# A two-layer hybrid backbone on one core: attention's float32 products issued in two groups of key blocks, a seventh place for a block, and another price of array changes in the kernel's clock model

## The chip, the core and the metric

The kernel runs on one core of a Trainium2 chip. The core has TensorE (PE, matrix products, into PSUM), VectorE (DVE), ScalarE (ACT), GpSimd (POOL) and SyncE (SP, which issues the DMAs). Each engine works through its own list of instructions in order and waits on semaphores for the others. The metric is the device time in microseconds of one execution.

## What is computed

Two layers on 1024 latent and 256 context tokens of width 1024, all in float32. In each layer one input projection feeds three groups of heads, whose outputs are gated, joined and projected out. The group that the change touches is windowed attention with 8 query heads of width 64 in two key-value groups, blocks of 128 tokens:

```python
def one_block(args):
    qn, kn, vn, mn = args
    s_loc = jnp.einsum('bqhgd,bkhd->bhgqk', qn, kn).astype(F32)
    s_loc = jnp.where(mn, s_loc, NEG_INF)
    s_ctx = jnp.einsum('bqhgd,bchd->bhgqc', qn, kc).astype(F32)
    s_sink = jnp.broadcast_to(sink_l[None, :, :, None, None], s_ctx.shape[:-1] + (1,))
    p = jax.nn.softmax(jnp.concatenate([s_sink, s_ctx, s_loc], axis=-1), axis=-1)
    p_ctx = p[..., 1:1 + nc].astype(vn.dtype)
    p_loc = p[..., 1 + nc:].astype(vn.dtype)
    return (jnp.einsum('bhgqc,bchd->bqhgd', p_ctx, vc)
            + jnp.einsum('bhgqk,bkhd->bqhgd', p_loc, vn))
...
y_l = jnp.concatenate([a_l, b_l, c_l], axis=-1) @ w_out
xl = xl + gate[:, None] * y_l
```

A latent block attends to the two context blocks and to itself and its neighbours, so to four or five key blocks; in layer 0 the two context blocks attend to the two context blocks alone. The other groups are a convolution module (31 taps, on DVE) and a gated linear attention in two directions (GLA).

## The kernel before

The program is written by a planner that runs when the kernel is built. Each piece of work is a generator, a "lane". It yields what it needs next: a flag, a free buffer, a free PSUM bank, or a time on the planner's clocks. `loop` takes the ready lane of the best priority and lets it issue; if none is ready, the planner's clock moves on. The clocks are kept by `Model`: `issue` adds the cost of each instruction to its engine's clock and notes when its result may be read. So the costs of the model decide the order of all engines, and the order stays as planned when the chip takes other times. `pick` also chooses by these clocks which engine does a copy or a subtraction. All instructions pass through one helper, so that the profile gives line 43 for all of them; they are told apart by the names of tiles.

A matmul that names a `tile_position` uses a part of the array's 128 columns. Three kinds do: PV of attention (64 columns), the GLA's states (32) and outputs and masks (64), and the modulation vectors (32). All other matmuls and the transposes use 128. In the model a matmul with `tile_position` costs its share of the columns and 29 ns.

Attention runs in units of one query block and one key-value group: 20 in layer 0, 16 in layer 1. `u_run` takes four probability buffers P of 644 columns, issues the scores of four heads (`u_score`), and each head's mask, maximum and exponential run in `u_head`. Then the rows are scaled, and for each key block four transposes (one a head) bring the probabilities into a PSUM bank. `u_ev` copies the bank into a place "PT" of 512 columns, on ACT or DVE. There are six such places, all in tile H1_0, made by `h1_keep`, which also holds the values `vst`. `u_pv` multiplies the transposed probabilities with the values, one key block after the other, into one bank O, two matmuls a block (output partitions 0 to 63 and 64 to 127), and frees the place after each block. A float32 matmul shows as two in the profile, so one block as four.

The SM buffers (14, and one more that holds the rotary table for a while) are divided during attention (`rsv`): nine wide ones of 644 columns for P and the mask, and the narrow ones SM9 to SM14 of 512 columns for the preparation of queries and keys, the gates and the output.

`out_tiles` is the output projection, in two lanes (`par` 0 and 1) that take every second block. Each splits the mixed activations of its block in a leading part `hi` and a correction `lo` (float32 as two parts). Lane 0 keeps half of `lo` in `ml`, a part of tile H1_1, for all blocks but the last four, and needs one SM buffer then; lane 1 needs two. Towards the end of layer 0 the tokens are normalised for layer 1 (`x_next`, `part_h`), which then starts with the first projection groups.

Of the kernel before, what the change touches and what calls it, by code (L numbers as in the profile page):

```python
# [30 lines left out]
def is_ap(x):  # L31
    return hasattr(x, "tensor") and hasattr(x, "ap")


class Engine:


    def __init__(self, model, name, e):
        self._m, self._n, self._e = model, name, e
# [9 lines left out]
class Model:  # L49
# [3 lines left out]
    def __init__(self, nc):  # L53
        self.nc = nc
        self.clock = dict(pe=0.0, act=0.0, dve=0.0, pool=0.0, sp=0.0, ring=0.0, dma=0.0)
        self.mem, self.memo = {}, {}
        self.end = self.cold = 0.0
        for n, a in (("pe", "tensor"), ("act", "scalar"), ("dve", "vector"), ("pool", "gpsimd"), ("sp", "sync")):
            setattr(self, a, Engine(self, n, getattr(nc, a)))

# [56 lines left out]
    def issue(self, e, op, a, k):  # L117
        out = a[0]
        outs = [x for x in (out, k.get("accum_out")) if is_ap(x)]
        ins = [x for x in list(a[1:]) + [v for n, v in k.items() if n != "accum_out"] if is_ap(x)]  # L120
        c = self.clock
        t = c[e]
        w = 2 if e == "pe" else 0
        rp, wp = [self.part(x) for x in ins], [self.part(x) for x in outs]
        for m, b in rp:
            t = max(t, m[w, b].max())
        for m, b in wp:
            t = max(t, m[1, b].max())
            if e != "pe":
                t = max(t, m[0, b].max())  # L130
        if e == "sp":
            c["sp"] = t + 50
            c["ring"] = max(c["ring"], t) + 475
            c["dma"] = max(c["dma"], c["ring"] + 625) + out.free_size() * 4 * out.partition_size() / 360.0
            t = c["dma"]
            near, far = 908, 1100
        else:
            x = self.cost(e, op, out, ins, len(outs) - 1)
            if e == "pe":
                if "tile_position" in k:  # L140
                    x = x * out.partition_size() / 128.0 + 29
                if t - c[e] > 3000 or t < 3000:
                    self.cold = t + 3800
                if t < self.cold:
                    x *= 2
            t += x
            c[e] = t
            near, far = (200, 200) if e == "pe" else (150, 370)
        for m, b in rp:
            m[1, b] = np.maximum(m[1, b], t + near)  # L150
        for m, b in wp:
            m[0, b] = np.maximum(m[0, b], t + near)
            m[2, b] = np.maximum(m[2, b], t + far)
        self.end = max(self.end, t + far)
# [10 lines left out]
class Hybrid:  # L165
# [71 lines left out]
    def memory(self):  # L237
# [10 lines left out]
        self.rt = self.tile(f"SM{NSM}", 512, F32)  # L248
        self.slots["PT"], self.slots["SF"] = [], []
        self.rsv, self.kept = False, None  # L250
# [30 lines left out]
    def get(self, cls, dt=F32, wide=False):  # L281
        x = min(self.choice(cls, wide), key=lambda y: (y[1] not in self.narrow and y[0] > 0, y[0]))
        self.slots[cls].remove(x)
        t = x[1] if cls in ("PT", "SF") else self.tile(x[1], 512 if x[1] in self.narrow else self.size[cls], dt)
        self.where[self.key(t)] = (cls, x[1], t)
# [258 lines left out]
    def h1_keep(self):  # L544
# [4 lines left out]
        for k in range(6):  # L549
            p = x[:, 768 + 512 * k:1280 + 512 * k]  # L550
            self.slots["PT"].append((self.nc.touched(p), p))

# [654 lines left out]
    def attn_start(self, l):  # L1207

        nc = self.nc
        self.kst = self.HC[:, 0:3072].rearrange("p (v s t) -> p v s t", v=2, s=2)  # L1210
        self.Q = [x.rearrange("p (h t) -> p h t", h=8) for x in (self.HC[:, 3072:4096], self.H1[1][:, 0:1024])]
        self.ml = self.H1[1][:, 3072:3584].rearrange("p (a b t) -> p a b t", a=2, b=2)
        yield self.need("SM", 1, 0, True), tuple(f"{x}{l}.{i}" for x in ("kv", "q0", "q1") for i in range(2, NT))
        self.rope_free()
        self.amask = self.sm(640)
        self.rsv = True
        nc.sync.dma_start(self.amask, self.I["amask"])
        self.go(self.gate_rows(l), 3)
        ctx = [0, 1] if l == 0 else []
        blocks = list(range(2, NT)) + ctx if CTXL else ctx + list(range(2, NT))  # L1220
        prev = None
        for n, i in enumerate(blocks):
            for kv in range(2):
                u = self.unit(l, n, i, kv, prev)
                self.units.append(u)
                u.lane = self.go(self.u_run(u), 2 + 0.01 * len(self.units))
                prev = u
        self.outs = self.go(self.out_proj(l, blocks), 8)
        done = set()
        for n, i in enumerate(blocks):  # L1230
            for t in self.keys(i):
                if t not in done:
                    done.add(t)
                    yield f"kv{l}.{t}", lambda: 0.0 if self.pre < 4 else None
                    self.pre += 1
                    self.go(self.kv_prep(l, t, blocks.index(t - 3) if t >= 6 else None), 1)
            yield f"q0{l}.{i}", f"q1{l}.{i}", lambda: 0.0 if self.pre < 4 else None
            self.pre += 1
            self.go(self.q_prep(l, n, i), 1)
# [69 lines left out]
    def unit(self, l, n, i, kv, prev):  # L1309
# [3 lines left out]
        u.keys = self.keys(i)  # L1313
        u.P, u.PT = {}, {}
        return u

    def u_run(self, u):
# [28 lines left out]
        for q in range(len(u.keys)):  # L1346
            yield self.bank_need("tr"), self.need("PT")
            tp = self.bank_get("tr")
            PT = self.get("PT")
            for h in range(4):  # L1350
# [49 lines left out]
    def u_pv(self, u):  # L1400

        nc = self.nc
        nk = len(u.keys)
        bank = None
        for q in range(nk):
            yield lambda: u.PT[q][1] if q in u.PT else None, (0.0 if q else self.bank_need("ac"))
            if q == 0:
                bank = self.bank_get("ac")
                O = bank[:, 0:256].rearrange("p (a t) -> p a t", a=2)
            PT = u.PT[q][0]  # L1410
            p4 = PT.rearrange("p (a b t) -> p a b t", a=2, b=2)
            for b in range(2):
                nc.tensor.matmul(O[64 * b:64 * b + 64], self.vst[:, self.kslot(u.keys[q]), u.kv], p4[:, :, b], start=(q == 0),
                                 stop=(q == nk - 1), tile_position=(0, 64 * b))
            self.free(PT)
        yield None, tuple(f"bg{u.l}.{2 + 2 * u.kv}.{j}.{self.hslot(u.i)[0]}" for j in (0, 1))
        c = col(u.i * 128)
        g = self.mix(slice(2 + 2 * u.kv, 4 + 2 * u.kv), slice(c, c + 128))
        nc.vector.tensor_tensor(g, O, g, op=ALU.mult)
        self.free(bank)  # L1420
        self.flag(f"u{u.key}")
# [52 lines left out]
    def out_tiles(self, l, blocks, par, lanes):  # L1474
        yield
        for n, i in list(enumerate(blocks))[par::2]:
            early = par == 0 and n < len(blocks) - 4
            lanes[par].prio = 8 + 0.01 * n
            if l == 0 and n >= len(blocks) - 2:
                a = 256 + 256 * par  # L1480
                hi = self.HC[:, 0:3072].rearrange("p (a c) -> p a c", a=4)[:, :, a:a + 256].rearrange("p a (b t) -> p a b t", b=2)
                free = f"sc{l}.{len(blocks) - 3}"
            else:
                a = 1024 + 1024 * par
                hi = self.H1[1][:, a:a + 1024].rearrange("p (a b t) -> p a b t", a=4, b=2)
                free = f"h1out{l}"
            yield (self.need("SM", 2 - early, 1), f"u{l}.{n}.0", f"u{l}.{n}.1", free, f"gb{l}",
                   f"ln{l}{self.hslot(i)[0]}", self.rest(hi), (self.rest(self.ml) if early else 0.0))
            m = [self.sm(512, F32R) for _ in range(2 - early)]
            lo = ([self.ml] if early else []) + [x.rearrange("p (a b t) -> p a b t", a=2, b=2) for x in m]  # L1490
            o = col(i * 128)
            for h in range(2):
                yield
# [144 lines left out]
    def phase_bc(self, l):  # L1638
        nc = self.nc
        yield self.attn  # L1640
        yield f"sc{l}.{NT - 1 if l == 0 else NT - 3}"
        self.rsv = False
        self.cap = dict(mm=0, tr=CAPC[0], ac=CAPC[1], md=MDC if l == 0 else 0)
        if l == 0:
            self.go(self.rope_load(), 3)
            for i in list(range(2, NT)) + [0, 1]:
                self.go(self.x_next(i), 1 + 0.01 * ((i - 2) % NT))
        yield tuple(u.lane for u in self.units), f"ml{l}.0", f"ml{l}.1"
        self.slots["SF"] = []
        if l == 0:  # L1650
            self.slots["PT"] = []
            self.h1_new(0, F32R)
        self.flag(f"hfree{l + 1}1")
        self.free(self.amask)
        yield self.outs
        self.flag(f"hfree{l + 1}0")
        self.flag(f"hfree{l + 1}2")
# [189 lines left out]
```

## Time and profile before

| | us |
|---|---|
| median of 3 runs (1331.18 to 1339.85) | 1332.32 |
| the profiled execution | 1333.02 |
| its span, first to last instruction | 1331.2 |
| TensorE busy | 1256.9 |
| DVE, ACT, POOL busy | 831.9, 563.6, 463.7 |
| PV, all 640 matmuls | 86.7 |

The profiled execution is one run with the hardware profiler on. A busy engine is one with an instruction in it; matmuls overlap each other, so that the time from one start to the next is shorter than the duration shown. In the order of time, neighbouring equal instructions are merged into one row with their count: start, us from the first start to the last end, engine, line, operation, output and inputs by tile names, shapes, count, and in brackets idle time ahead with its releaser. "128\*64" are rows and columns of the array in use. A wait is put down to the semaphore that came last.

### The profile page before, as it was taken

What the parts mean: (1) busy time and instruction counts of PE and PEld (TensorE: products, weight loads), DVE (VectorE), ACT (ScalarE), POOL (GpSimd) and SP (SyncE); (2) the same over time, 40 slices, a digit from 0 to 9 for tenths busy, and PEclk for the clock granted to TensorE, in tenths of its full rate; (3) what the DMA queues carried; (4) which work ended last, traced back from release to release, by engine and by line L of the source; (5) the groups of instructions that cost most, each with busy time, mean ns of one, the idle gap of its engine ahead of it and who ended that gap; (6) DMA issues with size and microseconds to landing.
All of it is one profiled execution on the core that took longest, in us unless ns stands there. A gap on an engine that the chain in (4) does not pass through costs nothing. (4 is left out here: it accounts for less than half of the span.)

```text
span 1331.2 us, 24579 instructions
## 1 busy us (share of the span) xinstructions
PE 1256.9 (94%) x9518; PEld 1064.3 (80%) x9518; DVE 831.9 (62%) x1566; ACT 563.6 (42%) x1279; POOL 463.7 (35%) x615
## 2 busy tenths in 40 slices
PE   5999988999999999999999799979999999999997
PEld 3678877888897777776899789878888777888877
DVE  5846896886364355466545578897854646675463
ACT  3721441254324465566513441521443346646541
POOL 1410054744132333534300231074751334445320
PEclk9999998999999999999999899999999999999999
DMA  9443114223014333323232521124231121231012
GB/s 330 147 153 104 48 41 105 60 68 96 25 32 143 101 98 95 97 76 104 82 118 88 198 74 61 41 58 110 80 83 32 50 85 45 66 117 53 1 64 72
DMA packets 113237, 116.49 MB, mean 88 GB/s; under 512 B 38464, under 2 KB 81760, under 8 KB 113120
## 3 DMA queue, kind: packets, MB, share of 16 engines
q1 hardware_dynamic: 113120, 114.92, 27.8%
q8 instruction: 75, 1.23, 0.4%
q14 instruction: 42, 0.34, 0.1%
HBM read 95.47 MB, written 19.42 MB: 86 GB/s over the span
## 5 line engine op out<-in xcount | busy, mean ns | idle before, releaser
L43 PE MATMUL ps<-H,WS 128*128 128x512 f32 x1344 | 337.9, 399 | 3.7 <-ACT U L43 1.7
L43 PEld LDWEIGHTS ps<-H,WS 128*128 128x128 f32 x1344 | 245.0, 189 | 63.0 <-issue 8.8
L43 PE MATMUL ps<-WS,H 128*128 128x256 f32 x1704 | 253.0, 290 | 0.0
L43 PEld LDWEIGHTS ps<-WS,H 128*128 128x128 f32 x1704 | 227.1, 194 | 11.4 <-issue 11.0
L43 ACT ACTIVATE SM<-ps 128x512 f32<-128x512 f32 (+3 forms) x144 | 71.4, 496 | 311.6 <-PE ps L43 270.3
L43 PE MATMUL ps<-idr,SM 128*128 128x128 f32 (+1 forms) x1076 | 151.3, 274 | 30.5 <-POOL SM L43 16.3
L43 DVE SCALAR_TENSOR_TENSOR mix<-U,small,mix 128x1295 f32<-128x1295 f32 (+1 forms) x120 | 176.8, 1514 | 0.0
L43 PEld LDWEIGHTS ps<-idr,SM 128*128 128x128 f32 (+1 forms) x1076 | 121.0, 142 | 63.1 <-POOL SM L43 20.5
L43 DVE CUSTOM_DVE_ANT_0 SM<-ps,SM,small 128x640 f32<-128x640 f32 (+2 forms) x128 | 102.2, 813 | 77.8 <-PE ps L43 73.5
L43 ACT ACTIVATE SM<-SM,stat 128x641 f32<-128x641 f32 (+2 forms) x144 | 110.6, 769 | 66.2 <-DVE stat L43 58.9
L43 ACT ACTIVATE H<-ps 128x512 f32<-128x512 f32 (+1 forms) x152 | 84.8, 598 | 74.1 <-PE ps L43 73.6
L43 POOL TENSOR_TENSOR tir<-tir,mhalf 128x1 f32<-128x1 f32 (+2 forms) x55 | 47.4, 866 | 182.3 <-DVE tir L43 157.3
L43 POOL TENSOR_TENSOR SM<-SM,SM 128x128 fp32r<-128x128 f32 (+3 forms) x56 | 56.5, 1017 | 134.0 <-ACT SM L43 110.0
L43 PE MATMUL ps<-H,H 128*128 128x256 f32 x552 | 97.4, 286 | 0.0
L43 POOL TENSOR_SCALAR SM<-SM,tir 128x640 f32<-128x640 f32 (+2 forms) x89 | 73.7, 842 | 53.3 <-DVE tir L43 42.2
L43 ACT ACTIVATE SM<-SM 32x128 f32<-32x128 f32 (+4 forms) x199 | 71.7, 368 | 40.1 <-DVE SM L43 33.7
L43 PE MATMUL ps<-H 128*64 128x256 f32 x640 | 86.7, 392 | 0.2 <-ACT H L43 0.2
L43 PE MATMUL ps<-SM,SM 128*32 128x128 f32 (+4 forms) x764 | 79.4, 288 | 7.1 <-ACT SM L43 3.5
L43 PEld LDWEIGHTS ps<-H,H 128*128 128x128 f32 x552 | 81.1, 189 | 2.8 <-issue 2.8
L43 POOL TENSOR_TENSOR SM<-SM,WR 128x256 f32<-128x256 f32 (+2 forms) x61 | 63.9, 1053 | 31.6 <-DVE SM L43 23.9
L43 POOL TENSOR_TENSOR WR<-SM,SM 128x256 f32<-128x256 f32 (+1 forms) x48 | 47.3, 1006 | 68.8 <-ACT SM L43 58.3
L43 PE MATMUL ps<-WS,SM 128*128 128x256 f32 x248 | 70.1, 283 | 1.1 <-DVE SM L43 1.1
(148 smaller groups left out, 2005.5 us busy)
## 6 DMA issues: line engine op xcount, KB each, us to landing
WR<-in_w_in_dram SPq DMA_DIRECT2D x80, 256.0 KB, 3.7
WR<-in_w_mod_dram SPq DMA_DIRECT2D x64, 256.0 KB, 3.0
WR<-in_w_out_dram SPq DMA_DIRECT2D x32, 256.0 KB, 3.3
SM<-vd SPq DMA_DIRECT2D x116, 64.0 KB, 2.4
x<-SM SPq DMA_DIRECT2D x20, 256.0 KB, 2.3
SM<-x SPq DMA_DIRECT2D x20, 256.0 KB, 4.7
qd<-SM SPq DMA_DIRECT2D x18, 256.0 KB, 2.3
mix<-in_x_dram SPq DMA_DIRECT2D x8, 512.0 KB, 8.0
```

The source lines that it names most:

```text
L43: r = getattr(self._e, op)(*a, **k)
```

## The change

Four things are changed.

- `u_pv` takes the key blocks in two groups, the first two and all the rest, and a group is issued when all its blocks are in their places. Units with two blocks have one group. The places are freed group by group.
- A seventh PT place is taken from the narrow SM buffers when attention starts (`attn_start`), and goes back to them at the end of layer 0's attention (`phase_bc`).
- Lane 1 of the output projection keeps half of its correction in H1_1 as well, next to lane 0's (`ml` becomes a list of two).
- In the clock model a matmul with `tile_position` has no 29 ns any more; instead the first one after a matmul without it costs 90 ns more, and the first one without it 180 ns more.

```diff
@@ Model.issue
             if e == "pe":
+                if ("tile_position" in k) != self.tiled:
+                    self.tiled = not self.tiled
+                    x += 90 if self.tiled else 180
                 if "tile_position" in k:
-                    x = x * out.partition_size() / 128.0 + 29
+                    x = x * out.partition_size() / 128.0
@@ attn_start
-        self.ml = self.H1[1][:, 3072:3584].rearrange("p (a b t) -> p a b t", a=2, b=2)
+        self.ml = [self.H1[1][:, 3072 + 512 * k:3584 + 512 * k].rearrange("p (a b t) -> p a b t", a=2, b=2) for k in range(2)]
...
+        self.pt7 = self.sm(512)
+        self.own7 = self.where[self.key(self.pt7)]
+        self.slots["PT"].append((0.0, self.pt7))
@@ u_pv
-        for q in range(nk):
-            yield lambda: u.PT[q][1] if q in u.PT else None, (0.0 if q else self.bank_need("ac"))
-            if q == 0:
+        for g in (range(2), range(2, nk))[:nk - 1]:
+            yield tuple((lambda q=q: u.PT[q][1] if q in u.PT else None) for q in g), (self.bank_need("ac") if bank is None else 0.0)
+            if bank is None:
                 bank = self.bank_get("ac")
                 O = bank[:, 0:256].rearrange("p (a t) -> p a t", a=2)
-            PT = u.PT[q][0]
-            p4 = PT.rearrange("p (a b t) -> p a b t", a=2, b=2)
-            for b in range(2):
-                nc.tensor.matmul(O[64 * b:64 * b + 64], self.vst[:, self.kslot(u.keys[q]), u.kv], p4[:, :, b], start=(q == 0),
-                                 stop=(q == nk - 1), tile_position=(0, 64 * b))
-            self.free(PT)
+            for q in g:
+                p4 = u.PT[q][0].rearrange("p (a b t) -> p a b t", a=2, b=2)
+                for b in range(2):
+                    nc.tensor.matmul(O[64 * b:64 * b + 64], self.vst[:, self.kslot(u.keys[q]), u.kv], p4[:, :, b], start=(q == 0),
+                                     stop=(q == nk - 1), tile_position=(0, 64 * b))
+            self.free(*[u.PT[q][0] for q in g])
@@ out_tiles
-            early = par == 0 and n < len(blocks) - 4
+            early = n < len(blocks) - 4
...
-            lo = ([self.ml] if early else []) + [x.rearrange("p (a b t) -> p a b t", a=2, b=2) for x in m]
+            lo = ([self.ml[par]] if early else []) + [x.rearrange("p (a b t) -> p a b t", a=2, b=2) for x in m]
@@ phase_bc, layer 0
             self.slots["PT"] = []
+            self.where[self.key(self.pt7)] = self.own7
+            self.free(self.pt7)
```

Since the model's costs set the order, the order of all engines changes, from the 23rd row of TensorE on. Two places on TensorE follow. A row there is one instruction or several equal ones: the output's tile, the inputs', the output's shape, the count (one float32 matmul counts once).

In the attention stage of layer 0, before: H_0 holds PT places and values, so that "64x256" is PV, one block in two matmuls; cst with WR is modulation, HC with HC are scores.

```order
L43 MATMUL ps_70<-WR_817_5777,cst 32x256 x2
L43 MATMUL ps_69<-H_0_534_4239 64x256 x2
L43 MATMUL ps_67<-HC_491 128x256 x2
L43 MATMUL ps_67<-HC_491 128x384 x2
L43 MATMUL ps_66<-HC_491 128x256 x2
L43 MATMUL ps_66<-HC_491 128x384 x2
L43 MATMUL ps_69<-H_0_534_4239 64x256 x2
```

And now, at the like place of a unit; SM_427 is the seventh place.

```order
L43 MATMUL ps_69<-H_0_527_4203 64x256 x2
L43 MATMUL ps_69<-SM_427_3820,H_0_527_4203 64x256 x2
L43 MATMUL ps_69<-H_0_527_4203 64x256 x2
L43 MATMUL ps_66<-HC_494 128x256 x2
L43 MATMUL ps_66<-HC_494 128x384 x2
L43 MATMUL ps_67<-HC_494 128x256 x2
L43 MATMUL ps_67<-HC_494 128x384 x2
```

Before, two blocks of a unit stand apart with scores between them; now the last three blocks of a unit follow each other, and the scores stand behind them.

At the start of layer 1, before, in TensorE's order: 128x512 is the first projection group (24 matmuls into bank ps_66), the rows with idr are transposes of the last tokens' normalised input.

```order
L43 MATMUL ps_66<-H_0_1005_7098,WS_1024_7296 128x512 x2
L43 MATMUL ps_66<-H_1_7_112,WS_1024_7296 128x512
L43 MATMUL ps_66<-H_0_1005_7098,WS_1024_7296 128x512
L43 MATMUL ps_69<-idr,SM_1047_7411 128x128 x4
L43 MATMUL ps_68<-idr,SM_1048_7412 128x128 x4
L43 MATMUL ps_66<-H_0_1005_7098,WS_1024_7296 128x512
L43 MATMUL ps_66<-H_1_7_112,WS_1024_7296 128x512
```

And now:

```order
L43 MATMUL ps_66<-H_0_1002_7094,WS_1022_7292 128x512 x2
L43 MATMUL ps_66<-H_1_7_112,WS_1022_7292 128x512
L43 MATMUL ps_66<-H_0_1002_7094,WS_1022_7292 128x512
L43 MATMUL ps_70<-idr,SM_1044_7405 128x128 x4
L43 MATMUL ps_68<-idr,SM_1045_7406 128x128 x4
L43 MATMUL ps_69<-idr,SM_1046_7412 128x128 x4
L43 MATMUL ps_70<-idr,SM_1047_7413 128x128 x4
L43 MATMUL ps_67<-H_0_1002_7094,WS_1022_7292 128x512
```

All 24 matmuls of the bank stand ahead of the first transposes, where 18 stood, and four pieces are transposed in a row instead of two.

More of the change, by code (lines that the diff above doesn't have):

```diff
@@ L57, in __init__ @@
         self.end = self.cold = 0.0
+        self.tiled = False
         for n, a in (("pe", "tensor"), ("act", "scalar"), ("dve", "vector"), ("pool", "gpsimd"), ("sp", "sync")):
@@ L1487, in out_tiles @@
             yield (self.need("SM", 2 - early, 1), f"u{l}.{n}.0", f"u{l}.{n}.1", free, f"gb{l}",
-                   f"ln{l}{self.hslot(i)[0]}", self.rest(hi), (self.rest(self.ml) if early else 0.0))
+                   f"ln{l}{self.hslot(i)[0]}", self.rest(hi), (self.rest(self.ml[par]) if early else 0.0))
             m = [self.sm(512, F32R) for _ in range(2 - early)]
-            lo = ([self.ml] if early else []) + [x.rearrange("p (a b t) -> p a b t", a=2, b=2) for x in m]
+            lo = ([self.ml[par]] if early else []) + [x.rearrange("p (a b t) -> p a b t", a=2, b=2) for x in m]
             o = col(i * 128)
```

## The prediction

> **What bounds the kernel now.** I read first the page's head with the busy times, then the chain that ended last, the waits of TensorE, the costliest groups, and last the order of time on TensorE in the attention stage of layer 0.
>
> ```profile
> span 1331.2 us, 24579 instructions
> ...
> PE 1256.9 (94%) x9518; PEld 1064.3 (80%) x9518; DVE 831.9 (62%) x1566; ACT 563.6 (42%) x1279; POOL 463.7 (35%) x615
> ```
>
> TensorE is busy for 94% of the span and nothing else for more than 62% (its weight loads run beside its own matmuls). So time is won in two ways only: TensorE is given less to do, or it waits less. Its waits, longest first:
>
> ```profile
> PE ps L43 <- POOL SM L43: 16.3, 12, 4.2
> PE ps L43 <- ACT SM L43: 14.9, 12, 6.9
> PE ps L43 <- DMA HC<-in_w_mod_dram: 12.0, 2, 11.6
> PE ps L43 <- DVE SM L43: 7.9, 7, 2.1
> PE ps L43 <- DVE stat L43: 6.7, 8, 2.4
> ```
>
> Columns are us in total, times, longest. Apart from the first load (12.0) these four releasers hold 45.8 us in 39 waits. Now the attention stages (the first two stretches) beside the two recurrent (GLA) stages:
>
> ```profile
> core 0: us, PE busy (x) PEld busy (x) DVE busy (x) ACT busy (x) POOL busy (x), PEclk, DMA share, GB/s
> 440.00:680.00 240.00, 234.94 (x1786) 183.30 (x1785) 127.05 (x302) 133.17 (x298) 91.59 (x167) 1.00 0.31 97
> 1080.00:1300.00 220.00, 211.99 (x1611) 178.67 (x1610) 129.84 (x269) 121.30 (x258) 90.20 (x142) 0.99 0.18 59
> 170.00:330.00 160.00, 148.03 (x1447) 132.93 (x1446) 126.49 (x176) 56.76 (x152) 90.96 (x83) 0.98 0.28 74
> 860.00:1020.00 160.00, 149.49 (x1389) 130.50 (x1388) 116.62 (x174) 57.56 (x150) 86.15 (x84) 0.98 0.26 72
> ```
>
> In attention TensorE stands idle for 5.1 us (240 - 234.94) and 8.0 us, so 13.1 us is all that a better order could win there by waiting less. The products of the attention weights with the values (PV, the matmuls that the change regroups) are this group:
>
> ```profile
> L43 PE MATMUL ps<-H 128*64 128x256 f32 x640 | 86.7, 392 | 0.2 <-ACT H L43 0.2
> ```
>
> 640 matmuls are 160 key blocks of four (two halves of the output, float32 in two passes). They wait 0.2 us in all: nothing is to be won from their own waits.
>
> **The price of an array change.** PV matmuls fill 64 of the 128 columns ("128*64"), the GLA's and modulation's fill 64 or 32, everything else 128. The order of time on TensorE (start, us, shape, count) shows what going in and out costs. I call a run of narrow matmuls between two full ones a visit.
>
> ```profile
> 586.64 0.54 PE L43 MATMUL ps<-idr,SM 128*128 128x128 f32 x4
> 587.11 1.08 PE L43 MATMUL ps<-H 128*64 128x256 f32 x8
> 588.12 1.45 PE L43 MATMUL ps<-HC 128*128 128x256 f32 x8
> ...
> 590.13 1.07 PE L43 MATMUL ps<-idr,SM 128*128 128x128 f32 x8
> 590.96 1.42 PE L43 MATMUL ps<-HC 128*128 128x256 f32 x8
> 592.31 0.65 PE L43 MATMUL ps<-H 128*64 128x256 f32 x4
> 592.89 0.66 PE L43 MATMUL ps<-idr,SM 128*128 128x128 f32 x4
> 593.48 0.65 PE L43 MATMUL ps<-H 128*64 128x256 f32 x4
> 594.06 0.50 PE L43 MATMUL ps<-H,H 128*128 128x256 f32 x2
> ...
> 597.28 0.63 PE L43 MATMUL ps<-WR,cst 128*32 128x256 f32 x4
> 597.83 0.65 PE L43 MATMUL ps<-H 128*64 128x256 f32 x4
> 598.41 1.44 PE L43 MATMUL ps<-HC 128*128 128x256 f32 x8
> 599.78 0.65 PE L43 MATMUL ps<-H 128*64 128x256 f32 x4
> ```
>
> From start to next start, one block takes 0.58 (592.31 to 592.89) and two blocks in one visit 1.01 (587.11 to 588.12). The second block adds 0.43, so 0.15 us of every visit is the change itself. The full neighbours stretch too: four transposes between two visits take 0.59 (592.89 to 593.48), eight among full work 0.83 (590.13 to 590.96), that is 0.42 for four: 0.17 more. With other neighbours:
>
> ```profile
> 506.97 0.92 PE L43 MATMUL ps<-HC,H 128*128 128x256 f32 x6
> 507.82 0.65 PE L43 MATMUL ps<-H 128*64 128x256 f32 x4
> ...
> 510.22 0.81 PE L43 MATMUL ps<-HC,H 128*128 128x256 f32 x6
> 510.86 1.06 PE L43 MATMUL ps<-idr,SM 128*128 128x128 f32 x8
> ```
>
> Six score matmuls between two visits take 0.85, among full work 0.64: 0.21 more. A visit so costs 0.15 + 0.17 = 0.32 to 0.15 + 0.21 = 0.36 us; where the neighbour hardly stretches (586.64 to 587.11, 0.47 against 0.42) it costs 0.20. I take 0.32, since transposes are the commonest neighbours of PV.
>
> **The change, part by part.**
>
> *Two groups a unit.* No matmul is added or removed (8294 matmul instructions in both orders). What counts is the number of visits. Counted over the whole order of TensorE there were 193 and are now 181; visits that hold PV fall from 80 to 57 (layer 0: 43 to 31, layer 1: 37 to 26), those with modulation go from 57 to 59, those of the GLA outputs and masks from 27 to 34, those of the states stay 32 (a few visits hold two kinds). 23 PV visits less by 0.32 are -7.4 us; 11 come back elsewhere, +3.5 us. Net 12 x 0.32 = **-3.8 us**, between 12 x 0.20 = -2.4 and 12 x 0.36 = -4.3. The array time of the blocks themselves (0.43 each) does not change. TensorE is the bound in attention, so the saving lies on the path; the seven GLA visits are added where TensorE idles 12.0 and 10.5 us, so some of them may cost nothing, and I charge them in full.
>
> *The wait the grouping adds.* Blocks 2 to the last of a unit now wait for the last one's eviction from PSUM (ACT or DVE). Behind the waiting matmul stand TensorE's next transposes and scores. In the order now the last group stands behind several plain matmuls after its last transposes, so the cover is other units' and layers' matmuls; the wait was 0.2 us for 640. I take 0. If the cover were gone, each of the 57 visits would wait for one eviction, ACT's or a slower one:
>
> ```profile
> L43 ACT ACTIVATE H<-ps 128x512 f32<-128x512 f32 (+1 forms) x152 | 84.8, 598 | 74.1 <-PE ps L43 73.6
> ```
>
> 57 x 0.6 = 34 us is the upper end, -0.2 the lower; I take the lower end's neighbour, 0, because the wait of 0.2 us comes from the order that had less between a block's transposes and its PV.
>
> *Places.* Attention blocks hold their places longer, hence the seventh place. It comes out of the narrow SM buffers: five are left of six during attention. The second output lane takes its correction term from the H1 tile instead of an SM buffer, which gives one back for all but the last four blocks. Neither adds an instruction. I take 0 and keep it as a rival.
>
> *Evictions and splits that change engine.* DVE has 1573 rows now against 1568, ACT 1090 against 1091, POOL 614 against 620, DMA issues 534 in both. At about 1 us each that is 5 us on engines busy for 62% and less: 0 on the path.
>
> *The prices in the clock model.* The model put 29 ns on each narrow matmul; now it puts 90 and 180 ns on going in and out, 0.27 us a visit, near the measured 0.32. Since every matmul's planned start moves, the whole order differs from its 23rd row on. That reshuffles the waits. I read one place, the largest wait of all, between the layers:
>
> ```profile
> 746.34 4.27 PE L43 MATMUL ps<-H,WS 128*128 128x512 f32 x18
> 757.50 1.97 PE L43 MATMUL ps<-idr,SM 128*128 128x128 f32 x8 [6.90 <-ACT SM L43]
> 759.12 2.91 PE L43 MATMUL ps<-H,WS 128*128 128x512 f32 x6
> 761.83 2.25 PE L43 MATMUL ps<-idr,SM 128*128 128x128 f32 x12
> ```
>
> 18 matmuls of the first projection group of layer 1 stood ahead of the wait for the last tokens' normalised input, six behind the first transposes. Now all 24 stand ahead. Six take 4.27/18 x 6 = 1.4 us at full rate, and fill that much of the 6.90 us. But four transposed pieces now come in a row, of which the last two may not have landed. So between 0 and -2.7 (759.12 to 761.83, what the six took there); I take **-1.4 us**.
>
> *Sum.* The profiled execution took 1333.0 us, of which 1331.2 are the span; the median of the runs is 1332.3. 1333.0 - 3.8 - 1.4 = **1327.8, so 1328 us**.
>
> *A rule beside a row.* The modulation matmuls (32 columns) at 597.28, with PV (64 columns) directly behind, take 0.55 us against 0.43 for a block within a visit. The Trainium skill, "TensorEngine Tiling (Array Packing)", Key Properties, says that changing the tiling mode, not only the tile, drains the engine. By it a run of modulation next to a run of PV is two visits, where my count and the clock model of the kernel see one. Three such neighbours stood in the old order and one stands now; by the rule 14 visits are saved, 4.5 us in place of 3.8, and the time would be 1327. The row's extra 0.12 speaks for part of it; the sum stays as it is.
>
> **The rivals.**
>
> *The order with true prices waits less.* If three quarters of the 13.1 us of idle time in the attention stages go as well, 9.8 us, the time is 1333.0 - 5.2 - 9.8 = **1318**. For it: the old prices understate a visit (0.06 for two matmuls of a block against 0.32), so the plan ran ahead of TensorE. Against it: a plan that runs ahead gives the other engines more time than planned, which makes waits rarer, not more frequent.
>
> *The reshuffle gives it back.* The order before attention changes as well, and TensorE idles 22.5 us in the two GLA stages, where seven visits are added. If those waits grow by a quarter, 5.6 us, the gain is gone: **1333**. For it: 45.8 us in 39 waits hang on what stands ahead of them.
>
> *Slower: the attention stage runs out of SM buffers.* With five narrow places and one kept free, the preparation of queries asks for two beside the gates' and output tails' ones. If each of the 18 query blocks of both layers comes late once, at the price of a wait for DVE's SM work (7.9/7 = 1.1 us), that is 20 us, and 1333.0 + 20 - 5.2 = **1348**. It decides from 12 of the 18 on. For it: the last PV of layer 0 stands 56 matmuls later in the order. Against it: that of layer 1 stands 54 earlier, and the lane that now takes H1 gives one buffer back.
>
> *That it doesn't do what it says* is part of the second: 160 blocks still make 57 PV visits, where 72 groups (two for each of 36 units) would allow that at most; grouping alone saved less than a third.
>
> **How the numbers follow.** The forecast as worked out, 1320 to 1336 by its price bounds and a few waits more or less, has 0.55; the better plan (1318) 0.17; the gain given back (1333) 0.20; the lack of buffers (1348) 0.08. The range is 1316 to 1341: it takes in the first three but for the better plan's low end, and leaves out the fourth. A measurement of this kernel tells about 1% from no change. Faster by over 1% than the median means under 1319.0: most of the better plan and the forecast's edge, 0.16. Slower by over 1% means over 1345.6: most of the fourth, 0.07. Within 1%: 0.77.
>
> **What would show it.** Right: runs of eight and twelve PV matmuls where runs of four stood, each visit still with its 0.15 and the stretched neighbours; PV's busy time under 86.7 us and its wait still near 0.2 us; between the layers a wait of about 5.5 us with 24 matmuls ahead of it. Wrong: a PV wait of microseconds (the grouping has no cover), transposes in attention that wait for DVE or ACT more than 13.1 us (buffers), or waits in the GLA stages well over 22.5 us (reshuffle). A place whose wait of 2 us or more is new would upset the sum, as would a visit that costs less among full work than among visits.

## The result

The changed kernel takes 1324.35 us (median of 8 runs, 1322.2 to 1328.14), the kernel before 1332.28 us in the same comparison (8 runs): a ratio of 0.9943, 95% interval 0.9924 to 0.9962. That is 7.6 us less (5.1 to 10.1), within 1%. The forecast was 1328, the range 1316 to 1341.

The head of the changed kernel's page, of the execution that took 1323.65 us:

```profile
span 1321.9 us, 24553 instructions
...
PE 1254.0 (95%) x9518; PEld 1066.9 (81%) x9518; DVE 838.4 (63%) x1571; ACT 561.2 (42%) x1280; POOL 452.9 (34%) x609
```

TensorE does the same 9518 matmuls in a span 9.3 us shorter, and its waits say where a part of that comes from (us in total, times, longest):

```profile
PE ps L43 <- POOL SM L43: 16.4, 11, 3.7
PE ps L43 <- DMA HC<-in_w_mod_dram: 12.1, 2, 11.7
PE ps L43 <- ACT SM L43: 9.7, 11, 3.4
PE ps L43 <- DVE SM L43: 4.4, 7, 1.4
PE ps L43 <- DVE H L43: 3.6, 4, 2.0
PE ps L43 <- DMA SM<-vd: 3.1, 5, 1.1
PE ps L43 <- DVE stat L43: 2.7, 5, 0.9
PE ps L43 <- DMA WR<-in_w_mod_dram: 2.1, 4, 1.1
PE ps L43 <- POOL H L43: 1.7, 2, 1.0
```

ACT, DVE and the softmax sums ("stat") hold TensorE 12.7 us less than before (14.9 + 7.9 + 6.7 to 9.7 + 4.4 + 2.7). New are DVE H and POOL H, 5.3 us. Three of these waits, at 535.45, 550.39 and 551.74, 3.7 us together, are for pieces of the output projection's weights that are not split yet when their matmul is due; the other 1.6 us are for copies of a PSUM bank into a PT place. All idle time ahead of TensorE's matmuls adds up to 66.3 us before and 59.9 now (the rows of this view, which leave out the shortest gaps, to 65.6 and 59.5).

The same four stretches as before (attention of layer 0 and 1, then the two GLA stages):

```profile
440.00:680.00 240.00, 230.69 (x1758) 182.38 (x1757) 127.84 (x301) 140.76 (x317) 92.73 (x168) 1.00 0.30 91
1080.00:1300.00 220.00, 217.23 (x1706) 189.37 (x1705) 140.08 (x299) 119.08 (x256) 84.87 (x140) 1.00 0.21 67
170.00:330.00 160.00, 149.31 (x1397) 134.51 (x1396) 126.09 (x162) 56.00 (x147) 92.24 (x84) 0.97 0.27 72
860.00:1020.00 160.00, 149.44 (x1350) 130.56 (x1348) 118.88 (x172) 58.38 (x151) 83.36 (x82) 0.98 0.27 72
```

In layer 1's attention the idle time of TensorE fell from 8.0 to 2.8 us, in layer 0's it rose from 5.1 to 9.3. The GLA stages hardly moved. Between marks that the traces have in common, the gain sits in one place (us; three of the versions that follow below stand beside):

| from | to | before | changed | lane 1 alone | grouping and place | all, old price |
|---|---|---|---|---|---|---|
| start | first PV of layer 0 | 445.8 | 449.9 | 446.6 | 449.0 | 447.6 |
| there | first 128x512 matmul of layer 1 | 300.5 | 302.2 | 295.7 | 295.2 | 291.0 |
| there | first PV of layer 1 | 341.0 | 337.4 | 340.0 | 343.6 | 343.9 |
| there | end of the last matmul | 236.0 | 224.4 | 231.9 | 225.8 | 226.6 |

Layer 1's attention and output gained 11.6 us; everything up to layer 1 lost 5.8 us, and the stretch from there to layer 1's first PV, which begins with the transition, gave 3.6 back. These are single executions. The first stretch took 449.9, 453.4 and 454.1 us in three that have the same order up to there (the changed kernel and two versions below), so a difference of some 4 us in one stretch says little; the 11.6 us are well over that.

PV itself, now under two names, since the seventh place is an SM buffer:

```profile
L43 PE MATMUL ps<-H 128*64 128x256 f32 x548 | 72.3, 388 | 0.7 <-ACT ps L43 0.3 <-DVE H L43 0.2 <-ACT H L43 0.2
...
L43 PE MATMUL ps<-SM,H 128*64 128x256 f32 x92 | 14.3, 389 | 0.0
```

548 + 92 are the 640 matmuls of before, waiting 0.7 us against 0.2. The two busy times add up to 86.6 us, but that counts twice the time in which matmuls of both groups overlap; with the intervals of the trace joined, PV is busy for 81.9 us against 86.7, 4.8 less. In the order of time they stand in longer runs:

```profile
490.86 1.52 PE L43 MATMUL ps<-H 128*64 128x256 f32 x12
492.31 0.85 PE L43 MATMUL ps<-HC 128*128 128x256 f32 x4
```

Three blocks take 1.45 us from start to next start: the 0.15 us once and three times 0.43, as before. The transition to layer 1:

```profile
752.12 5.63 PE L43 MATMUL ps<-H,WS 128*128 128x512 f32 x24
761.13 3.70 PE L43 MATMUL ps<-idr,SM 128*128 128x128 f32 x16 [3.38 <-ACT SM L43]
764.48 1.88 PE L43 MATMUL ps<-H,WS 128*128 128x512 f32 x6
```

All 24 matmuls stand ahead of the wait, which is 3.38 us in place of 6.90; the four pieces in a row found their data there. From the first of these matmuls to the first transpose it is 9.0 us, against 11.2 before: counted from there, the input itself came 2.1 us earlier.

### The profile page after: what moved, and what is told of

It is laid out like the page before. It is cut to its first block, busy times and chain, and to the rows that moved or that the text cites. A ratio compares the mean times of both kernels' runs of the same rounds, so it can differ in the third digit from the quotient of the medians.

```text
span 1321.9 us, 24553 instructions
## 1 busy us (share of the span) xinstructions
PE 1254.0 (95%) x9518; PEld 1066.9 (81%) x9518; DVE 838.4 (63%) x1571; ACT 561.2 (42%) x1280; POOL 452.9 (34%) x609
## 4 chain that ended last, share of the span: by engine, by line
PE 69%; DVE 8%; POOL 6%; DMA 6%; issue 5%; ACT 4%; SPq 1%; POOLq 0%; DVEq 0%; ACTq 0%
PE ps L43 69%; POOL SM L43 4%; DVE SM L43 3%; ACT SM L43 2%; DVE mix L43 2%; DMA WR<-in_w_out_dram 2%; DVE H L43 2%; DMA WR<-in_w_mod_dram 2%; POOL WR L43 1%; DMA WR<-in_w_in_dram 1%; DVE WS L43 1%; SPq L43 1%; DMA HC<-in_w_mod_dram 1%; ACT H L43 1%; ACT L43 0%
## 5 line engine op out<-in xcount | busy, mean ns | idle before, releaser
L43 PEld LDWEIGHTS ps<-H,WS 128*128 128x128 f32 x1344 | 244.3, 189 | 63.8 <-issue 12.2
L43 PEld LDWEIGHTS ps<-WS,H 128*128 128x128 f32 x1744 | 230.4, 195 | 10.0 <-issue 9.5
L43 ACT ACTIVATE SM<-ps 128x512 f32<-128x512 f32 (+2 forms) x164 | 82.7, 509 | 343.6 <-PE ps L43 289.3
L43 DVE SCALAR_TENSOR_TENSOR mix<-U,small,mix 128x1295 f32<-128x1295 f32 (+1 forms) x120 | 180.9, 1549 | 0.0
L43 DVE CUSTOM_DVE_ANT_0 SM<-ps,SM,small 128x640 f32<-128x640 f32 (+2 forms) x128 | 102.7, 813 | 60.1 <-PE ps L43 53.5
L43 POOL TENSOR_TENSOR SM<-SM,SM 128x128 fp32r<-128x128 f32 (+3 forms) x59 | 60.9, 1041 | 158.7 <-ACT SM L43 107.9
L43 ACT ACTIVATE H<-ps 128x512 f32<-128x512 f32 (+1 forms) x129 | 72.7, 596 | 65.2 <-PE ps L43 63.7
L43 PEld LDWEIGHTS ps<-H,H 128*128 128x128 f32 x592 | 83.8, 189 | 5.5 <-DVE H L43 2.2
L43 ACT ACTIVATE SM<-SM 32x128 f32<-32x128 f32 (+3 forms) x194 | 70.3, 369 | 38.3 <-DVE SM L43 30.0
L43 PE MATMUL ps<-H 128*64 128x256 f32 x548 | 72.3, 388 | 0.7 <-ACT ps L43 0.3
L43 POOL TENSOR_TENSOR SM<-SM,WR 128x256 f32<-128x256 f32 (+2 forms) x60 | 61.8, 1036 | 20.0 <-DVE SM L43 13.8
L43 DVE TENSOR_TENSOR WS<-WR,WS 128x512 fp32r<-128x512 f32 x66 | 60.7, 932 | 5.2 <-ACT WS L43 3.6
L43 PEld LDWEIGHTS ps<-SM,SM 128*64 128x64 f32 (+2 forms) x764 | 45.4, 127 | 20.0 <-ACT SM L43 6.1
```

The costliest lines, as they stand in the source:

```text
L43: r = getattr(self._e, op)(*a, **k)
```

## The experiments

Each kernel was run in alternation with the kernel before. The theories are: V, the time follows the number of visits; P, true prices make a better plan; L, lane 1's buffer is what counts; S, any other plan scatters the time.

| version | median us | ratio to before, 95% | visits | TensorE's waits | clock | waits for tile H |
|---|---|---|---|---|---|---|
| before | 1332.3 | | 193 | 66.3 | 0.987 | 0.2 |
| changed | 1324.4 | 0.9943 (0.9924 to 0.9962) | 181 | 59.9 | 0.991 | 5.5 |
| price alone | 1364.0 | 1.0226 (1.0196 to 1.0256) | 207 | 78.0 | 0.979 | 14.0 |
| all but the price | 1321.1 | 0.9904 (0.9878 to 0.9931) | 173 | 60.3 | 0.990 | 1.8 |
| changed, lane 1 on SM | 1336.8 | 1.0025 (1.0007 to 1.0043) | 181 | 67.1 | 0.985 | 8.0 |
| changed, visits split | 1366.4 | 1.0233 (1.0201 to 1.0264) | 273 | 56.1 | 0.987 | 4.2 |
| lane 1 alone | 1323.7 | 0.9947 (0.9927 to 0.9967) | 191 | 57.8 | 0.989 | 0.2 |
| grouping and place alone | 1324.5 | 0.9946 (0.9928 to 0.9964) | 173 | 60.2 | 0.986 | 2.5 |
| before with 32 ns | 1331.9 | 1.0010 (0.9993 to 1.0028) | 198 | 60.1 | 0.985 | 2.4 |
| changed with 100 and 190 ns | 1349.5 | 1.0141 (1.0113 to 1.0169) | 177 | 71.4 | 0.974 | 7.9 |
| all but the price, TensorE 3% slower in the plan | 1356.6 | 1.0190 (1.0158 to 1.0223) | 167 | 80.8 | 0.976 | 8.6 |
| the same, 3% faster | 1339.3 | 1.0053 (1.0031 to 1.0076) | 174 | 70.5 | 0.980 | 8.1 |
| all but the price, 32 ns | 1346.8 | 1.0115 (1.0086 to 1.0145) | 174 | 72.0 | 0.981 | 13.0 |
| all but price and seventh place | 1321.0 | 0.9920 (0.9891 to 0.9950) | 172 | 59.2 | 0.987 | 1.5 |

Visits are counted in the order, waits are all idle time ahead of TensorE's matmuls, the clock is the mean granted one of the profiled execution, the last column the waits for DVE, POOL or ACT on tile H. The kernel before had medians of 1332.3 to 1333.1 us in the comparisons; differences to it below are taken within one comparison, those between two versions from their medians.

**The new prices alone.**

```diff
+                if ("tile_position" in k) != self.tiled:
+                    self.tiled = not self.tiled
+                    x += 90 if self.tiled else 180
                 if "tile_position" in k:
-                    x = x * out.partition_size() / 128.0 + 29
+                    x = x * out.partition_size() / 128.0
```

> The kernel before with the new array prices in the clock model alone; PV block by block, six places, lane 1 as before. Its order has 207 visits of narrow matmuls against 193 before and 181 in the changed kernel. Theory V (the time follows the number of visits at 0.32 us each): 14 visits more, +4.5 us, 1336.8 against the 1332.3 of before. Rival P (true prices give a better plan, and the gain of the change is theirs): about 1324 to 1327, with the idle time of TensorE in layer 1's attention falling from 8.0 us towards 2.8 as in the changed kernel.

1364.0 us, 31 us slower than before. Both theories fall: V allowed 4.5 us, P a gain. The place that shows it best is the output projection of layer 0, between 540 and 560 us, where TensorE comes to pieces of the weights one after the other before they are there:

```profile
542.47 0.39 PE L43 MATMUL ps<-H,H 128*128 128x256 f32 x1 [0.79 <-DVE H L43]
543.59 1.09 PE L43 MATMUL ps<-H,H 128*128 128x256 f32 x7 [0.73 <-DVE H L43]
547.20 0.58 PE L43 MATMUL ps<-H,H 128*128 128x256 f32 x1 [2.04 <-DVE H L43]
548.60 1.86 PE L43 MATMUL ps<-H,H 128*128 128x256 f32 x7 [0.82 <-POOL H L43]
552.07 0.58 PE L43 MATMUL ps<-H,H 128*128 128x256 f32 x1 [0.75 <-DVE H L43]
```

Behind the 2.04 us the matmuls take longer (0.58 for one at 547.20 against 0.39 at 542.47, both behind a wait): the granted clock is 0.98 from 540 to 547 us and 0.50 from 547 to 560. So this place costs the waits and half the clock behind them. Over the whole trace, waits for such pieces are 12.2 of the 14.0 us on tile H.

**All of the change but the prices.**

```diff
-                if ("tile_position" in k) != self.tiled:
-                    self.tiled = not self.tiled
-                    x += 90 if self.tiled else 180
                 if "tile_position" in k:
-                    x = x * out.partition_size() / 128.0
+                    x = x * out.partition_size() / 128.0 + 29
```

> The changed kernel with the old price (29 ns on each narrow matmul); grouping, seventh place and lane 1 stay. 173 visits. Theory V: 20 visits fewer than before, -6.4 us, 1325.9 or a little under the changed kernel's time with its 181 visits (1324.4 - 2.6 = 1321.8). Rival P: without the true prices the gain is gone, 1330 to 1333.

1321.1 us: within 1 us of the 1321.8 that V gives from the changed kernel, and 4.8 under the 1325.9 that it gives from the kernel before. Its median is 3.2 us under the changed kernel's, but the intervals of the two ratios overlap. The gain of the change does not need the prices.

**Lane 1 back on SM buffers.**

```diff
-            early = n < len(blocks) - 4
+            early = par == 0 and n < len(blocks) - 4
```

> The changed kernel with lane 1 of the output projection back on two SM buffers. 181 visits, as in the changed kernel. Theory V: 1324.4, within 2 us. Rival L (the shorter waits of layer 1 come from the buffer that lane 1 gives back): with five narrow buffers and none given back the waits of TensorE between 1080 and 1300 us return to 8 us or more, 1330 or over.

1336.8 us, 12.4 us slower than the changed kernel at the same 181 visits. V falls as the whole account, L holds in size. In place it holds in part: TensorE idles 7.3 us between 1080 and 1300 us, where 8 or more were expected and the changed kernel has 2.8, and layer 1's attention and output take 229.1 us against 224.4; but the stretch from the first PV to layer 1 takes 311.5 us against 302.2.

**Lane 1 alone, on the kernel before.**

```diff
-            early = par == 0 and n < len(blocks) - 4
+            early = n < len(blocks) - 4
...
-            lo = ([self.ml] if early else []) + [x.rearrange("p (a b t) -> p a b t", a=2, b=2) for x in m]
+            lo = ([self.ml[par]] if early else []) + [x.rearrange("p (a b t) -> p a b t", a=2, b=2) for x in m]
```

> The kernel before with lane 1's correction in H1_1 and nothing else of the change. 191 visits against 193. Theory V (visits alone, 0.32 us each): 1332.3 - 0.6, about 1332. Theory L (lane 1's buffer is worth by itself what the changed kernel lost without it, 12 us): 1320 to 1323.

1323.7 us with two visits fewer: 8.7 us come from this edit alone, with the plan that it draws; V falls, L's 1323 is nearly met. On TensorE the order is that of the kernel before up to 521 us. TensorE idles less in both attention stages:

```profile
440.00:680.00 240.00, 236.57 (x1796) 184.85 (x1796) 128.67 (x307) 134.12 (x299) 91.97 (x168) 1.00 0.32 99
1080.00:1300.00 220.00, 215.28 (x1661) 183.03 (x1662) 135.73 (x277) 118.82 (x253) 86.82 (x138) 1.00 0.19 61
```

3.4 us and 4.7 us, where it was 5.1 and 8.0. Its waits for DVE's SM and stat work, 7.9 + 6.7 us before, are now

```profile
PE ps L43 <- DVE SM L43: 4.3, 5, 1.6
PE ps L43 <- DVE stat L43: 2.9, 6, 0.9
```

7.4 us less, of the 8.5 that all its waits lost.

**Grouping and the seventh place, without lane 1 and prices.** The edit is that of all but the prices, with `early` as before.

> Grouping and the seventh place, with the old price and lane 1 on two SM buffers. 173 visits. Theory V: 20 visits fewer than before, -6.4 us, 1326. Theory L (the gain of the version with the old price is lane 1's): 1331 to 1334. Both apart, each with half: 1328 to 1330.

1324.5 us, 7.9 us less than before with 20 visits fewer. V expected 6.4; L and the halves fall. With lane 1 added it becomes 1321.1: the two gains, 8.7 and 7.9, give 12.0 together.

**Without the seventh place.**

```diff
-        self.pt7 = self.sm(512)
-        self.own7 = self.where[self.key(self.pt7)]
-        self.slots["PT"].append((0.0, self.pt7))
...
-            self.where[self.key(self.pt7)] = self.own7
-            self.free(self.pt7)
```

> Grouping and lane 1 with the old price, without the seventh place (six places, six narrow buffers). 172 visits. If grouping needs the seventh place: 1327 or more, with waits of TensorE for ACT and DVE in attention. If not: 1319 to 1323.

1321.0 us: no difference. With the old price the groups fit into six places; with the new prices it was not tried.

**The price of a visit, in an order that is held.** A full matmul on two columns of zeros is put between the blocks of each group, past the clock model, so that every other instruction keeps its place. It adds zero to the product.

```diff
             for q in g:
+                if q > g[0]:
+                    nc.nc.tensor.matmul(bank[:, 0:2], self.idf, self.cst[:, 0, 2:4], start=False, stop=False)
                 p4 = u.PT[q][0].rearrange("p (a b t) -> p a b t", a=2, b=2)
```

> The changed kernel's order with one full matmul of two columns, which adds zeros to the product, between the blocks of each PV group, unknown to the clock model so that nothing else moves: 92 of them, each splitting a visit in two. Theory V: 92 x 0.32 = 29 us, and the added matmul's own two passes at about 0.11 us each, 20 us: 1373. If a visit costs only the 0.15 us inside it: 92 x 0.36 = 33 us, 1357. If the array change is hidden behind the weight loads: 1344.

1366.4 us, 42 us more, for 92 added matmuls: 0.46 each. The trace has the same:

```profile
498.80 0.65 PE L43 MATMUL ps<-H 128*64 128x256 f32 x4
499.38 0.38 PE L1419 MATMUL ps<-cst,idr 128*128 128x2 f32 x2
499.69 0.65 PE L43 MATMUL ps<-H 128*64 128x256 f32 x4
500.27 0.38 PE L1419 MATMUL ps<-cst,idr 128*128 128x2 f32 x2
500.59 0.65 PE L43 MATMUL ps<-H 128*64 128x256 f32 x4
501.17 0.50 PE L43 MATMUL ps<-HC 128*128 128x256 f32 x2
```

From 498.80 to 501.17 three blocks and two of the added matmuls take 2.37 us, in one visit three blocks take 1.45: 0.46 for each split. The added matmul's own share I read from like ones in the changed kernel:

```profile
504.63 0.50 PE L43 MATMUL ps<-sel,SM 128*128 128x2 f32 x4
504.99 0.48 PE L43 MATMUL ps<-WS,H 128*128 128x256 f32 x2
```

Two passes are 0.36 / 2 = 0.18 us, so 0.28 are left for the change of the array there and back; that is an estimate, since the like ones stand among full work. With 0.11 a pass, as the expectation had it, it would be 0.24. The expected 1373 was seven too high, since it had 0.54 for each split (0.32 + 0.22). A part of the price lies in PV's own records: with 92 visits more PV is busy for 103.3 us in place of 81.9.

**Is it the price, or any other plan?** Five versions change nothing but a number in the clock model.

```diff
-                    x = x * out.partition_size() / 128.0 + 29
+                    x = x * out.partition_size() / 128.0 + 32
```

on the kernel before,

> The kernel before with 32 ns in place of 29 on each narrow matmul in the clock model: no part of the change, only another plan. 198 visits against 193. Theory V: +1.6 us, 1334. Theory S (any other plan scatters the time by many microseconds, so that single differences of the order of 5 us tell little about the edit): it differs from before by 4 us or more in either direction beside the 1.6.

and on all of the change but the prices,

> Grouping, seventh place and lane 1 with 32 ns in place of 29 on each narrow matmul: the version with the old price in another plan. 174 visits against 173. Without scatter of the plan: 1321 to 1322. With scatter of the size that 100 and 190 ns showed under the new price: off by 8 us or more, and then nothing is known of the price's own effect.

then other prices in the changed kernel,

```diff
-                    x += 90 if self.tiled else 180
+                    x += 100 if self.tiled else 190
```

> The changed kernel with 100 and 190 ns for the array changes in place of 90 and 180: the same edit with another plan. 177 visits against 181. Theory V: 1324.4 - 1.3 = 1323. Theory S (scatter of the plan): it differs from the changed kernel by 4 us or more. Theory P (a price nearer to the measured 0.32 us plans better): 1320 or less.

and every cost of TensorE by 3% up (as shown) or down (0.97), on all of the change but the prices.

```diff
+                x *= 1.03
                 if t - c[e] > 3000 or t < 3000:
```

> Grouping, seventh place and lane 1 with the old price (1321.1), and every TensorE cost in the clock model 3% higher: the plan thinks TensorE slower, without any price on array changes. 167 visits. Theory K (a plan in which TensorE is slower leaves the other engines less time, so that TensorE waits more on the chip, and this is what the new prices did): 1328 or more, waits and half-clock time of TensorE over the 60 and 27 us of the version with the old price. Rival N (the loss belongs to the array prices alone): with six visits fewer 1319 to 1323.

> The same with every TensorE cost in the clock model 3% lower. 174 visits. Theory K: 1321 or less, waits of TensorE at or under 60 us and half-clock time at or under 27 us. Rival N: 1321 with scatter to both sides, waits not fewer.

3 ns more leave the kernel before where it was (1331.9), and cost the other version 25.7 us (1346.8). 10 ns more on the prices cost 25.1 us (1349.5). 3% slower costs 35.5 us, 3% faster 18.2. K falls, since it wanted a gain for the faster plan, and N falls, since the slower plan needs no price to lose. S misses on the kernel before, where it wanted 4 us or more, and holds on the versions with the change. It is lopsided: of five such plans four are far slower and none is clearly faster. The two views that tell them from the good ones are the clock and the waits:

```profile
440.00:680.00 240.00, 229.20 (x1710) 182.18 (x1709) 123.37 (x293) 128.15 (x287) 93.38 (x165) 0.96 0.29 88
1080.00:1300.00 220.00, 210.85 (x1553) 175.55 (x1552) 140.82 (x289) 125.02 (x268) 90.70 (x155) 0.99 0.20 61
```

This is the plan with TensorE 3% slower; its granted clock is 0.96 in layer 0's attention, where those under 1333 us have 0.99 or 1.00. The waits of all but the price, with 32 ns, longest first:

```profile
PE ps L43 <- POOL SM L43: 14.6, 10, 3.6
PE ps L43 <- DMA HC<-in_w_mod_dram: 12.1, 2, 11.7
PE ps L43 <- ACT SM L43: 8.5, 12, 2.5
PE ps L43 <- DVE SM L43: 8.3, 13, 1.2
PE ps L43 <- DVE H L43: 6.9, 7, 1.9
PE ps L43 <- POOL H L43: 6.1, 7, 1.2
```

Of the 13.0 us on tile H, 12.1 are for weights that are late for the output projection, 6.6 in layer 0 and 5.5 in layer 1. In the table, every version under 1333 us but the changed kernel waits 2.5 us or less for tile H, every one of 1336 us or more but the one with split visits 7.9 us or more; the changed kernel stands between them with 5.5, and the split one, which has its order, with 4.2. Why a plan of other costs brings the matmuls ahead of their weights was not tried.

**One account for thirteen of the fourteen.** From a profiled span I take the waits, the time lost to the clock, (1 - clock) x span, and 0.32 us a visit. Before: 1331.2 - 66.3 - 17.3 - 61.8 = 1185.8. Price alone: 1360.7 - 78.0 - 28.6 - 66.2 = 1187.9. TensorE 3% slower: 1351.6 - 80.8 - 32.4 - 53.4 = 1185.0. All but price and seventh place: 1316.0 - 59.2 - 17.1 - 55.0 = 1184.7. The split version has the work of 92 matmuls more and is left out; of the other thirteen the remainder lies between 1181.8 and 1193.0, while the spans lie between 1316 and 1361. So the three terms carry most of the large differences, not those of a few us. They overlap a little, since the clock also drops inside waits (in the kernel before it is 0.84 from 745 to 757 us, where TensorE stands for 6.90). The changed kernel is at 1321.9 - 59.9 - 11.9 - 57.9 = 1192.2: its terms fell by 6.4 + 5.4 + 3.9 = 15.7 us, its span by 9.3. The 6.4 us between them are in no term, and what they are stays open; lane 1 on SM, whose order on TensorE is the same up to 521 us, has them too (1193.0).

## Why the prediction was right, and where it was not

The time fell to the side and within the range that were forecast, and 7.6 us lie near the 4.5 us forecast against the median. The working was right only in part: two terms that had been put at nothing are not nothing in the runs (lane 1's place, 8.7 to 12.4 us less, and the new prices, 3.3 to 31 us more), and that they partly cancel, so that the total came out close, is luck.

- *Visits, -3.8 us.* The price of 0.32 was bounded by 0.20 and 0.36 and measures 0.28 (0.46 less 0.18) in a held order: 12 visits are 3.4 us. That the time is charged with visits at all is shown by the split version, for those of PV; the price of the GLA's and modulation's was not measured. They account for less than half of the gain, and they do not rank the versions: the one with the fewest, 167, takes 1356.6 us. Whether modulation next to PV makes one visit or two, 0.7 us in the sum, no run tells. The 72 groups set against the 57 visits should be 68, since four units of layer 0 have one group; 160 blocks less 68 groups are the 92 matmuls that the split version adds.
- *The added wait, 0.* Right: 0.7 us for 640 matmuls. That the seventh place would be needed for it was wrong, with the old price at least: nothing is lost without it there.
- *Places, 0.* This step failed. I costed lane 1's correction in H1_1 at nothing and kept the buffers as a rival for a loss. It alone makes the kernel before 8.7 us faster, and without it the changed kernel is 12.4 us slower. On the kernel before, 7.4 us went from the 14.6 us of waits for DVE's SM and stat work. In the changed kernel without it these waits are 8.0 us against 7.1, and it is those for POOL SM, for DMA WR and for tile H that are longer, by 2.4, 3.0 and 2.5 us. So both edits show what the place is worth together with the plan it draws, and not how a buffer ends a wait: that stays open. A plan alone moved the time by 18 us and more in four of five cases, though never clearly down.
- *The prices in the model, neutral or better.* This step failed too. The rival that true prices plan better had 0.17; prices alone lose 31 us, and in all three pairs that differ in them the version with the new prices is slower (by 3.3, 12.3 and 31 us). But four of the five other changes of a number cost 18 to 36 us, so what is shown is that this plan is touchy, not that these prices are worse than others.
- *The transition, -1.4 us.* The mechanism was right, the size not: the wait fell by 3.5 us (6.90 to 3.38). I counted the six matmuls that moved ahead and bounded the term at 2.7. They are 1.4 us of the 3.5 (24 take 5.63 where 18 took 4.27); the other 2.1 are the input that came earlier, which the sum did not have. The four pieces in a row did not wait. The gain belongs to this plan: with prices of 100 and 190 ns 18 matmuls stand ahead again, and the wait is 4.93 us.
- *What would show it.* Runs of eight and twelve, the wait of PV near zero, its busy time under 86.7 us (81.9) and 24 matmuls ahead of the transition came as said. The wait there is 3.38 us and not about 5.5. One sign of being wrong came too: a new wait of 2 us, the 2.03 us for a weight piece at 550.39.
- *The rivals.* That the reshuffle gives the gain back had 0.20 and named the GLA stages; these stayed at 10.7 and 10.6 us idle. It was the output projection's weights in layer 0 that gave back 3.7 us. The lack of buffers as a cause of slowness had 0.08 and is what the version without lane 1's place shows, at 1336.8 in place of 1348.

## What to carry to other kernels

Where a planner's costs write the order, an edit is at least two edits: what it does, and the plan that it happens to draw. Hold the order and change one thing (an instruction put past the model), and run the same edit with numbers that should not matter, before a difference is put down to the edit; here 3 ns moved the time by 0 or by 26 us. On a busy TensorE look first at waits and at the granted clock, and count a change of the array there and back at about 0.3 us, as here.

## What the hardware showed that I had not expected

A wait of less than 2 us can have a slower clock behind it. In the kernel before, TensorE waited 1.84 us ahead of 722.24, with a granted clock of 1.00 from 715 to 722 us, and then had a clock of 0.66 over the next five microseconds:

```profile
722.24 0.63 PE L43 MATMUL ps<-WS,HC 128*128 128x256 f32 x2 [1.84 <-ACT SM L43]
```

```profile
722.00:727.00 5.00, 4.76 (x27) 4.77 (x28) 3.76 (x9) 4.25 (x12) 1.28 (x1) 0.66 0.35 129
```

(1 - 0.66) x 5 = 1.7 us, nearly the wait again. A wait of 2.03 us in the changed kernel, ahead of 550.39, had no such end (two matmuls behind it take 0.40 as ever). The Trainium skill, "TensorE: Matmul & The Clock Gate", in "Why this matters for your kernels", advises against idle gaps of more than about 3 us. These traces agree above that length and show drops below it: in the thirteen of the account, from 20 us on, 50 of 51 gaps of 3 us or more have a mean granted clock under 0.95 over the 4 us behind them, and so have 38 of 88 gaps of 1.2 to 2.6 us. What tells the 38 from the others was not tried. The account above needs the term: it runs from 11.9 us in the changed kernel to 35.0 us with prices of 100 and 190 ns.
